# A start of its own for each pair's split weights, at every multiple of 4 bytes from 4 to 252

## The chip, the cores and the metric

The kernel runs on one core of one Trainium2 chip. The metric is device time in microseconds, from the first to the last instruction of one execution as the host sees it, as a median over runs.

## What is computed

The reference is a two-layer trunk on a sequence of 512 frames of width 1024, in float32. Each layer normalises x, projects it by one wide matrix, runs two recurrences in chunkwise form, merges them, and adds three residual blocks:

```
h  = rmsnorm(x, norm1_g);  z = h @ w_in + b_in            # 12296 columns
A  = sigmoid(mo) * headnorm(mlstm(q, k, v, i, f))         # 4 heads, dk = dv = 256
B  = silu(rg) * headnorm(retention(rope(rq), rope(rk), rv))   # 4 heads, dk = 256, dv = 512
x += (sigmoid(gm) * (A @ w_bm) + sigmoid(gr) * (B @ w_br)) @ w_out
x += relu(rmsnorm(x) @ w_ff1 + b_ff1)^2 @ w_ff2 + b_ff2
x += sigmoid(rmsnorm(x) @ w_pe_gate) * (p @ w_pe)
```

A last rmsnorm gives the output. Nearly all the arithmetic is dense products of a 1024-row weight matrix with the 512 frames.

## The kernel before, in words

**Three products for one.** Activations lie transposed, 128 features on the partitions and frames along the free axis. TensorE multiplies in a reduced form of float32 (float32r), so each operand is split in two: `hi`, the value as ScalarE writes it in that form, and `lo`, what is left, made by VectorE as the source minus `hi` (`split`, L308 to L310: L309 is ScalarE's part, L310 VectorE's). Each product is then three matmuls into one PSUM accumulation: hi by hi, hi by lo, lo by hi.

**Units.** The work is a list of units (`unit_list`), one per weight block, in a fixed order. There are three kinds that matter here:

- T8 units: a 1024 x 128 weight block, stationary, against all 512 frames. 8 feature blocks by 3 matmuls of 128 x 512 (`mm3`, L488 to L490).
- WIDE units: a 1024 x 1024 block in which the weights are the moving operand (L583 to L585).
- PAIR units, 75 of them: a 1024 x 256 block computed by one level of Strassen's scheme. It has 7 products, each of 4 feature blocks by 3 matmuls with the weights stationary and 256 frames or sums of frames moving: 84 matmuls of 128 x 256 (`run_pair`, L539 to L541). The weights of a pair come in four pieces: A, B and C of 1024 columns, D of 512.

The seventh product, P4 with piece D, is held back and issued in the middle of the next unit, after its second product.

**The feed.** Raw weights come by SyncE's DMA queue into one of 4 buffers `wr` (L413 to L428). Sums of weight blocks that the scheme needs are made beforehand in DRAM by accumulating DMAs on GpSimd's queue (L367), or by VectorE in the buffers (L467 to L474). `prep_next` (L431 to L475) takes a piece, splits it from `wr` into a tile `both` of the pool `w` (3 buffers; one more for D), and leaves two views of the tile, `hi` and `lo`, for TensorE. It runs a few pieces ahead of the products (`ready`).

**Where the split weights lie in their tile.** The tile is `2 * w + SLACK` words of 4 bytes per partition, with w = 1024 (512 for D) and `SLACK` = 64. The two views start `o` words in, and lie one behind the other:

```
both = pl.tile([P, 2 * w + SLACK], F32R, name=f"w{n}_{nm}", **kw)          # L443
o = 2 if units[n][0] == "PAIR" or pl is not wpool else 0                   # L444
out_ = [both[:, o + a * w:o + a * w + w] for a in range(1 if gates else 2)]
```

So pairs, and the last 4 units (which have 256 frames moving too), start 8 bytes into their tile, and all other units at its start. In the program as built every tile of split weights starts 32 bytes past a multiple of 64 in its partition, and so do the tiles of activations, of scores (`ph`, `pl`) and of values (`vh`, `vl`). A block of 128 weights is 512 bytes, so all blocks of one piece have the same distance from a multiple of 64.

Two other kinds of matmul have about 256 columns moving: the scores of the heads (`scores`, L817 to L836: tiles `l0m1s` and the like, in their shorter rows), and the product of scores and values of the mLSTM (`attend`, L838 to L845: `l0m2a`, `l0m3a`), with scores stationary and 258 columns of values moving. Values of two heads share a tile: head 2 starts at its word 0, head 3 at its word 258 (1032 bytes).

Of the kernel before, what the change touches and what calls it, by code (L numbers as in the profile page):

```python
# [124 lines left out]
def is_wide(g):  # L125
    return g[1][:2] in ("rv", "rw")
# [7 lines left out]
def has_t2(g):  # L134

    return is_full(g) or g[1][0] == "f"
# [117 lines left out]
def build(ctx, tc, ins, out):  # L254
    nc = tc.nc
    ve, ac, gp, te = nc.vector, nc.scalar, nc.gpsimd, nc.tensor
    units = [u for i in range(L) for u in unit_list(i)]
    NU = len(units)

    def pool(name, bufs, **kw):  # L260
        return ctx.enter_context(tc.tile_pool(name=name, bufs=bufs, **kw))

    def phase(name, side, bufs=1):
        return tc.alloc_tile_pool(name=name, bufs=bufs, side=side, reuse_waits="tile")
# [5 lines left out]
    wpool = pool("w", PIECES)  # L270
# [31 lines left out]
    def ps(name):  # L302
        return psum.tile([P, T], F32, name=name, tag="ps")

    def tmp(name, dt=F32):
        return cur["tmp"].tile([P, T], dt, name=name, tag="t", bufs=cur["ntmp"])

    def split(src, hi_ap, lo_ap):  # L308
        a = ac.activation(hi_ap, src, AF.Copy)  # L309
        return a, ve.tensor_sub(lo_ap, src, hi_ap.bitcast(F32))  # L310

    def in_order(kind, *new):

        for a, b in zip(cur.get(kind, ()), new):
            tc.add_manual_dep(b.ins, a.ins.name, ORDER, reason="order of the weights")
        cur[kind] = new
# [4 lines left out]
    for g, v in groups().items():  # L321
        index[g] = len(index)
        src, n, w = ("wwide", 2, UN) if is_wide(g) else ("wpairs", len(v), Q)
# [63 lines left out]
    def full(n):  # L387
        return units[n][0] in ("PAIR", "WIDE") and is_full(units[n][1])
# [10 lines left out]
    def halves(n):  # L399

        return [slice(0, Q), slice(Q, UN)] if n == 1 else [slice(0, UN)]

    def fill_raws(most=RAWS + 1):
        while at["load"] < len(loads) and len(raws) + len(kept) < most:
            n, x = loads[at["load"]]
            r = None
            if n in cur["room"] and cur["more"] not in raws:
                cur["more"] = n, x
                r = cur["low"].tile([P, UN], F32, name=f"wr{at['load']}", tag="wrx", bufs=1)
            elif len(raws) - (cur["more"] in raws) >= RAWS:  # L410
                break
            raws[n, x] = r = r or wpool.tile([P, UN], F32, name=f"wr{at['load']}", tag="wr", bufs=RAWS)
            if x:  # L413
                _, g, p = units[n]
                assert made.get((g, x[1] if is_wide(g) else p)) == 2 * len(MADE_OF(g)), (g, p, made, at["unit"])
                if is_wide(g):
                    in_order("load", nc.sync.dma_start(r, block(g, x[0])[x[1]]))
                else:
                    for k, y in enumerate(PIECE[x][:1] if x == "B" and not has_t2(g) else PIECE[x]):
                        in_order("load", nc.sync.dma_start(r[:, k * Q:(k + 1) * Q], block(g, y)[p]))  # L420
            elif units[n][0] == "IF":
                eng = nc.sync if n else nc.scalar
                eng.dma_start(r[:, 0:64], ins["wif"][n * L // NU])
            else:
                w = ins["wstream"][at["whole"]]
                for c in halves(n):
                    in_order("load", nc.sync.dma_start(r[:, c], w[:, c]))
                at["whole"] += 1  # L428
            at["load"] += 1

    def prep_next():  # L431
        n, x = order[at["prep"]]
        at["prep"] += 1
        fill_raws()

        w = Q if x == "D" else UN
        pl = cur["last"] if n >= NU - LAST else wpool
        kw = {"tag": "d", "bufs": 1} if x == "D" else {"tag": "l", "bufs": LAST} if pl is not wpool else {
            "tag": "w", "bufs": PIECES}
        wide = isinstance(x, tuple)  # L440
        nm = f"{x[0]}{x[1]}" if wide else x
        gates = units[n][0] == "IF"
        both = pl.tile([P, 2 * w + SLACK], F32R, name=f"w{n}_{nm}", **kw)  # L443
        o = 2 if units[n][0] == "PAIR" or pl is not wpool else 0  # L444
        out_ = [both[:, o + a * w:o + a * w + w] for a in range(1 if gates else 2)]
        r = formed.pop((n, x), None)
        if r is None:
            r = raws.pop((n, x))
        if gates:
            z = out_[0]  # L450
            gp.memset(z.bitcast(F32), 0.0)
            z = z.rearrange("p (k g c) -> p k g c", g=4, c=32)
            split(r[:, 0:64].rearrange("p (k g c) -> p k g c", g=2, c=H), z[:, :, 0:2, 0:H], z[:, :, 2:4, 0:H])
        elif x == 0:
            with tc.high_priority(AHEAD if n < 10 and units[n][0] == "V" or units[n][1:] == SOON else 0):
                for c in halves(n):
                    in_order("prep", *split(r[:, c], *[a[:, c] for a in out_]))
        else:
            in_order("prep", *split(r[:, :w], *out_))
        pieces[n, x] = out_  # L460
        if full(n) or not wide and x in ("A", "C") and has_t2(units[n][1]):
            pass
        elif x == "A" or wide and x[0] == "t2":
            kept[n, x] = r
        elif x == "C":

            ve.tensor_tensor(raws[n, "B"][:, Q:], kept.pop((n, "A"))[:, Q:], r[:, :Q], OP.add)  # L467
        elif x == "B":

            ve.tensor_tensor(r[:, :Q], r[:, :Q], r[:, Q:], OP.add)  # L470
            formed[n, "D"] = r
        elif wide and x[0] == "B21":
            t = cur["br"].tile([P, UN], F32, name=f"t4{n}_{x[1]}", tag=("ph", "pl")[x[1]])
            ve.tensor_tensor(t, kept.pop((n, ("t2", x[1]))), r, OP.add)  # L474
            formed[n, ("t4", x[1])] = t  # L475

    def ready(k):
        while at["prep"] < min(len(order), k + 1):
            prep_next()
# [12 lines left out]
    def t8(act, name):  # L492

        _, wh, wl = unit("T8")
        o = ps(name)
        for k in range(KT):
            s = slice(k * P, (k + 1) * P)
            mm3(o, wh[:, s], wl[:, s], act[0][k], act[1][k], k == 0, k == KT - 1)
            if k == 3:
                flush()  # L500
            if k in (2, 5):
                pace()
        return o
# [480 lines left out]
    for i in range(L):  # L984
        act_side, ph_side = ("right", "left") if i == 0 else ("left", "right")
        xa = n1.act
        if i:
            cur["low"] = phase(f"low{i}", ph_side)
            cur["tmp"], cur["ntmp"] = cur["low"], NTMP
            cur["room"] = range(i * NU // L, i * NU // L + room)  # L990
        cur["br"] = phase(f"br{i}", ph_side)
# [315 lines left out]
        for d in range(4):  # L1307
            o = t8(xa, f"l{i}m0z{d}") if d else oz
# [116 lines left out]
        for c in range(KT):  # L1425
# [4 lines left out]
            u = tmp(f"l{i}bml{c}")  # L1430
            nc.scalar.dma_start(u, bm_dram[i, c])
            o = t8(yr, f"l{i}br1{c}")
# [37 lines left out]
        for c in range(KT):  # L1470
            o = t8((mh, ml), f"l{i}wo{c}")
# [144 lines left out]
        for c in range(KT - LAST if last else KT):  # L1616
            o = t8(n3.act, f"l{i}pg{c}")
# [44 lines left out]
    for a, n in enumerate(nn):  # L1662
        for c in range(KT - LAST, KT):
            _, wh, wl = ws[c - KT + LAST]
            o = ps(f"pl{a}{c}")[:, :256]
# [21 lines left out]
    x_pool.release()  # L1687
    assert at["unit"] == NU and at["prep"] == len(order) and not pieces and not raws and at["load"] == len(loads) and not kept and not formed and at["step"] == len(steps)

# [117 lines left out]
```

## Time and profile before

| | |
|---|---|
| median of 3 runs | 2301.65 us (2300.31 to 2305.29) |
| the profiled execution | 2302.19 us |
| its span, first to last instruction | 2300.5 us |
| granted TensorE clock | 0.998 |
| DVE, ACT, POOL busy | 76%, 55%, 27% |

In a row of a timeline stand the start in us from the span's beginning, the duration in us, the engine, the line, the operation and what it writes and reads. Matmuls are pipelined and their ends are modelled, so the distance between two starts tells what one costs, and its duration doesn't. In a row of groups stand the line, engine, operation, output and inputs, shapes, count, then busy time in us and the mean of one in ns, then the idle time before them with what ended it. PEld is the loading of the stationary operand, which overlaps the matmul before.

### The profile page before, as it was taken

The numbers are of one execution on the slowest core, as the hardware profiler recorded it, in microseconds if no ns is written. First come the engines' busy times: TensorE is split into PE (matmuls) and PEld (weight loads), VectorE is DVE, ScalarE is ACT, GpSimd is POOL, SyncE is SP. The second block draws the span as 40 slices with busy tenths as digits, with TensorE's granted clock in tenths as the row PEclk, the third lists the DMA queues.
The fourth block names the chain that finished last, engine by engine and source line by source line (L and its number), as shares of the span: only waits on it lengthen the run. The fifth ranks groups of instructions, "written<-read, shape, count | busy, mean of one in ns | idle before, by whom it ended". The sixth has DMA issues, their size and how long they took to land.

```text
span 2300.5 us, 36407 instructions
## 1 busy us (share of the span) xinstructions
PE 2277.2 (99%) x13532; PEld 2020.8 (88%) x13532; DVE 1759.0 (76%) x2690; ACT 1266.5 (55%) x1835; POOL 616.2 (27%) x984
## 2 busy tenths in 40 slices
PE   9999999999999999999999999999999999999998
PEld 7888899888888899999888888988888888999997
DVE  7877767886676878788779687777867678787785
ACT  6766544554554546556557564445545446566564
POOL 3332222223124322223432332221232242111112
PEclk9999999999999999999999999999999999999999
DMA  6776787787789888888886768876877898878741
GB/s 211 189 195 175 243 234 215 209 235 211 233 228 268 220 229 229 239 239 210 227 227 183 196 177 250 232 213 220 228 221 208 244 266 217 246 233 232 236 161 56
DMA packets 187890, 499.33 MB, mean 217 GB/s; under 512 B 26352, under 2 KB 29808, under 8 KB 187712
## 3 DMA queue, kind: packets, MB, share of 16 engines
q0 software_dynamic: 57520, 188.53, 36.9%
q1 hardware_dynamic: 114496, 280.97, 36.2%
q10 hardware_dynamic: 15696, 27.50, 3.6%
q8 instruction: 106, 1.74, 0.3%
q14 instruction: 72, 0.59, 0.1%
HBM read 478.03 MB, written 194.51 MB: 292 GB/s over the span
## 4 chain that ended last, share of the span: by engine, by line
PE 85%; DVE 7%; ACT 2%; issue 2%; DMA 2%; POOL 1%; SPq 0%; DVEq 0%; ACTq 0%; POOLq 0%
PE l0f L488 1%; PE l0f L489 1%; PE l0f L490 1%; PE l0br L488 1%; PE l1br L488 1%; PE l1br L490 1%; PE l0br L490 1%; PE l1br L489 1%; PE l0br L489 1%; DVE w_B L310 1%; PE l1f L488 1%; PE l1f L490 1%; PE l1f L489 1%; DVE w_C L310 1%; PE l0pg L488 1%
## 5 line engine op out<-in xcount | busy, mean ns | idle before, releaser
L309 ACT ACTIVATE w<-wr 128x1024 fp32r<-128x1024 f32 (+1 forms) x193 | 199.7, 1042 | 125.9 <-issue 28.5
L310 DVE TENSOR_TENSOR w<-wr,w 128x1024 fp32r<-128x1024 f32 (+1 forms) x193 | 233.8, 1214 | 45.3 <-ACT w L309 44.7
L309 ACT ACTIVATE w_B<-wr 128x1024 fp32r<-128x1024 f32 x123 | 130.4, 1060 | 150.5 <-PE l0bm L490 13.1
L310 DVE TENSOR_TENSOR w_B<-wr,w_B 128x1024 fp32r<-128x1024 f32 x123 | 150.0, 1221 | 55.0 <-ACT w_B L309 54.5
L309 ACT ACTIVATE w_C<-wr 128x1024 fp32r<-128x1024 f32 x75 | 79.3, 1057 | 66.8 <-issue 9.6
L310 DVE TENSOR_TENSOR w_C<-wr,w_C 128x1024 fp32r<-128x1024 f32 x75 | 92.4, 1233 | 25.0 <-ACT w_C L309 21.0
L309 ACT ACTIVATE w_A<-wr 128x1024 fp32r<-128x1024 f32 x75 | 79.0, 1054 | 46.6 <-DMA wr<-wpairs 4.4
L310 DVE TENSOR_TENSOR w_A<-wr,w_A 128x1024 fp32r<-128x1024 f32 x75 | 91.6, 1222 | 14.2 <-ACT w_A L309 12.0
L309 ACT ACTIVATE w_t<-wr 128x1024 fp32r<-128x1024 f32 x56 | 59.1, 1059 | 61.8 <-PE l0g2va L585 6.3
L309 ACT ACTIVATE w_D<-wr 128x512 fp32r<-128x512 f32 x75 | 47.3, 631 | 81.6 <-DVE wr L470 26.7
L310 DVE TENSOR_TENSOR w_t<-wr,w_t 128x1024 fp32r<-128x1024 f32 x56 | 68.4, 1221 | 19.7 <-ACT w_t L309 19.1
L488 PE MATMUL l0f<-l0n2h,w 128*128 128x512 f32 x176 | 68.7, 390 | 0.0
L490 PE MATMUL l0f<-l0n2h,w 128*128 128x512 f32 x176 | 68.5, 389 | 0.0
L489 PE MATMUL l0f<-l0n2l,w 128*128 128x512 f32 x176 | 68.5, 389 | 0.0
L310 DVE TENSOR_TENSOR w_D<-wr,w_D 128x512 fp32r<-128x512 f32 x75 | 51.7, 689 | 15.1 <-ACT w_D L309 14.6
L367 POOL DMA_DIRECT2D s30t<-wpairs x24 | 16.8, 700 | 91.9 <-PE l1o20a L541 9.0
L490 PEld LDWEIGHTS l0f<-l0n2h,w 128*128 128x128 f32 x176 | 33.0, 188 | 7.0
L488 PEld LDWEIGHTS l0f<-l0n2h,w 128*128 128x128 f32 x176 | 33.0, 188 | 6.5
L489 PEld LDWEIGHTS l0f<-l0n2l,w 128*128 128x128 f32 x176 | 33.0, 188 | 6.4
L488 PE MATMUL l1f<-l1n2h,w 128*128 128x512 f32 x96 | 37.6, 391 | 0.0
L490 PE MATMUL l1f<-l1n2h,w 128*128 128x512 f32 x96 | 37.4, 390 | 0.0
L489 PE MATMUL l1f<-l1n2l,w 128*128 128x512 f32 x96 | 37.4, 389 | 0.0
(5796 smaller groups left out, 9085.3 us busy)
## 6 DMA issues: line engine op xcount, KB each, us to landing
wr<-wstream SPq DMA_DIRECT2D x189, 512.0 KB, 4.9
wr<-wpairs SPq DMA_DIRECT2D x225, 256.0 KB, 4.1
wr<-wwide SPq DMA_DIRECT2D x48, 512.0 KB, 4.6
s3t<-wwide POOLq DMA_DIRECT2D x24, 256.0 KB, 4.3
s6t<-wwide POOLq DMA_DIRECT2D x24, 256.0 KB, 5.2
s18t<-wwide POOLq DMA_DIRECT2D x24, 256.0 KB, 5.1
s21t<-wwide POOLq DMA_DIRECT2D x24, 256.0 KB, 5.1
s24t<-wpairs POOLq DMA_DIRECT2D x24, 256.0 KB, 5.7
```

The source lines that it names most:

```text
L309: a = ac.activation(hi_ap, src, AF.Copy)
L310: return a, ve.tensor_sub(lo_ap, src, hi_ap.bitcast(F32))
L367: dma = gp.dma_start(piece(g, x, p, q), piece(g, MADE[x][a], p, q), max_dma_last_dim=4096, **kw)
L488: te.matmul(o, sh, mh, start=first, stop=False)
L489: te.matmul(o, sh, ml, start=False, stop=False)
L490: cur["mm"] = te.matmul(o, sl, mh, start=False, stop=last)
```

## The change

The start `o` of a pair's pieces is no longer 2 for all pairs. The q-th pair of the program (counted from 0) takes `1 + 25 * q % 63`, that is 1 + ((25 q) mod 63) words: 1, 26, 51, 13, 38, 63, 25 and so on. The first 63 pairs take each whole number from 1 to 63 once, the last 12 take those of the first 12 again. All four pieces of a pair, hi and lo, share its start. The slack of 64 words already holds this, so tiles, buffers and addresses of all else stay where they were. On each engine the instructions and their order are the same, row for row.

```
@@ -256,6 +256,7 @@
     units = [u for i in range(L) for u in unit_list(i)]
     NU = len(units)
+    start_of = {n: 1 + 25 * q % 63 for q, n in enumerate(n for n, u in enumerate(units) if u[0] == "PAIR")}
@@ -441,7 +442,7 @@
         both = pl.tile([P, 2 * w + SLACK], F32R, name=f"w{n}_{nm}", **kw)
-        o = 2 if units[n][0] == "PAIR" or pl is not wpool else 0
+        o = start_of[n] if units[n][0] == "PAIR" else 2 if pl is not wpool else 0
         out_ = [both[:, o + a * w:o + a * w + w] for a in range(1 if gates else 2)]
```

Of the 75 starts 38 are odd numbers of words, and one (q = 58) is the 2 of before. Eight are multiples of 32 bytes, three of them of 64.

More of the change, by code (lines that the diff above doesn't have):

```diff
@@ L258, in build @@
     NU = len(units)
+    start_of = {n: 1 + 25 * q % 63 for q, n in enumerate(n for n, u in enumerate(units) if u[0] == "PAIR")}
     def pool(name, bufs, **kw):
@@ L443, in prep_next @@
         both = pl.tile([P, 2 * w + SLACK], F32R, name=f"w{n}_{nm}", **kw)
-        o = 2 if units[n][0] == "PAIR" or pl is not wpool else 0
+        o = start_of[n] if units[n][0] == "PAIR" else 2 if pl is not wpool else 0
         out_ = [both[:, o + a * w:o + a * w + w] for a in range(1 if gates else 2)]
```

## The prediction

> **What bounds the kernel now.** I read the page first (span, engines, chain), then timelines of TensorE, because what the change can touch is the step from one matmul's start to the next.
>
> ```profile
> span 2300.5 us, 36407 instructions
> PE 2277.2 (99%) x13532; PEld 2020.8 (88%) x13532; DVE 1759.0 (76%) x2690; ACT 1266.5 (55%) x1835; POOL 616.2 (27%) x984
> PEclk9999999999999999999999999999999999999999
> PE 85%; DVE 7%; ACT 2%; issue 2%; DMA 2%; POOL 1%; SPq 0%; DVEq 0%; ACTq 0%; POOLq 0%
> ```
>
> TensorE is busy 99% of the span at full clock and makes 85% of the chain that ended last. So the kernel is a row of matmuls end to end, and a nanosecond on each of the pairs' 75 x 84 = 6300 matmuls is 6.3 us, 0.27% of the time. About 0.2% (4.6 us) is what a measurement of this kernel can tell from no change. The profiled execution took 2302.19 us, its span and 1.7 us around it; the median of the runs is 2301.65, 0.02% less.
>
> What does a pair's matmul cost now? This is the timeline of TensorE at the first matmul of two pairs in a row, in a stretch without waits:
>
> ```profile
> 838.63 0.28 PE L539 MATMUL l0o02a<-l0hh,w_A 128*128 128x256 f32 x1
> ...
> 848.34 0.28 PE L539 MATMUL l0o03a<-l0hh,w_A 128*128 128x256 f32 x1
> ```
>
> Between the two lie 84 matmuls (72 of the one pair, and the 12 of P4 that the pair before left): 9.71 us / 84 = 115.6 ns. The last units, whose weights also start 8 bytes in, have the same step:
>
> ```profile
> 2267.77 0.28 PE L489 MATMUL pl<-l1n3l,w 128*128 128x256 f32 x1
> ...
> 2269.39 0.28 PE L488 MATMUL pl<-l1n3h,w 128*128 128x256 f32 x1
> ```
>
> 14 steps in 1.62 us: 115.7 ns. Weights at the tile's start with 512 frames moving:
>
> ```profile
> 129.09 0.39 PE L488 MATMUL l0m2z<-l0xnh,w 128*128 128x512 f32 x1
> ...
> 131.13 0.39 PE L488 MATMUL l0m2z<-l0xnh,w 128*128 128x512 f32 x1
> ```
>
> 9 steps in 2.04 us, 226.7 ns. The 256 columns more cost 111.1 ns, 0.43 ns a column. A load of weights has a price of its own, seen where the moving operand has only 2 columns (the last of these 8 matmuls runs between the two loads):
>
> ```profile
> 769.37 0.95 PE L710 MATMUL l0n2ss<-ones_r,l0n2sum 128*128 128x2 f32 x8
> ...
> 770.15 0.19 PEld L488 LDWEIGHTS l0f<-l0n2h,w 128*128 128x128 f32 x1
> 770.26 0.19 PEld L489 LDWEIGHTS l0f<-l0n2l,w 128*128 128x128 f32 x1
> ```
>
> Loads follow each other 110 ns apart there. So with 256 columns the moving stream (111) and the next load (110) are about equally long and run side by side, and the pairs' 115.6 is some 5 ns above either. Two streams that read SBUF at once and are both close to the bound: here a start can matter.
>
> **Does it, in this trace?** Two groups of matmuls, alike but for the distance between their two operands, answer. In both the scores are stationary, at 32 bytes past a multiple of 64, with 258 columns of values moving. The values of `l0m2a` start at 32 too; those of `l0m3a` start 1032 bytes later, so at 40.
>
> ```profile
> 205.00 0.28 PE L488 MATMUL l0m2a<-l0m1vh,l0m2ph 128*128 128x258 f32 x1
> ...
> 208.48 0.28 PE L490 MATMUL l0m2a<-l0m1vh,l0m2pl 128*128 128x258 f32 x1
> ...
> 240.82 0.28 PE L488 MATMUL l0m3a<-l0m1vh,l0m3ph 128*128 128x258 f32 x1
> ...
> 244.27 0.28 PE L490 MATMUL l0m3a<-l0m1vh,l0m3pl 128*128 128x258 f32 x1
> ```
>
> Each is 29 steps: 3.48 us or 120.0 ns with equal starts, 3.45 us or 119.0 ns with the weights 8 bytes behind the values. Less 0.9 ns for the 2 columns more that is 119.1 and 118.1 at 256 columns. The scores, equal starts and 256 columns, lie near that, though the stretch is short and follows longer rows:
>
> ```profile
> 118.80 0.28 PE L488 MATMUL l0m1s<-l0m1qh,l0m1kh 128*128 128x256 f32 x1
> ...
> 120.10 0.28 PE L490 MATMUL l0m1s<-l0m1qh,l0m1kl 128*128 128x256 f32 x1
> ```
>
> 11 steps in 1.30 us, 118.2 ns. So three distances of weights from moving operand have a price: 0 bytes 119.1 ns, 8 behind 118.1, 8 ahead (the pairs now) 115.6.
>
> **The change part by part.** Nothing is added, removed or moved in any engine's order; only addresses change, for three kinds of access.
>
> *ScalarE writes hi, VectorE reads hi and writes lo.* At the tile's start (group `w`, mostly T8) and at 8 bytes (`w_A`) the splits cost the same:
>
> ```profile
> L309 ACT ACTIVATE w<-wr 128x1024 fp32r<-128x1024 f32 x189 | 198.1, 1055 | 125.9 <-issue 28.5 <-PE l0m1vp L809 10.3 <-PE l1m1vp L809 10.3
> L309 ACT ACTIVATE w_A<-wr 128x1024 fp32r<-128x1024 f32 x75 | 79.0, 1054 | 46.6 <-DMA wr<-wpairs 4.4 <-PE l0bm L490 4.4 <-issue 3.9
> L310 DVE TENSOR_TENSOR w<-wr,w 128x1024 fp32r<-128x1024 f32 x189 | 232.0, 1230 | 45.3 <-ACT w L309 44.7
> L310 DVE TENSOR_TENSOR w_A<-wr,w_A 128x1024 fp32r<-128x1024 f32 x75 | 91.6, 1222 | 14.2 <-ACT w_A L309 12.0 <-PE l0r1brqa L541 0.7 <-PE l1r1brqa L541 0.7
> L1043 DVE SCALAR_TENSOR_TENSOR l0m00cv<-l0m00z,bc,l0m00cv x3: 741/743/743, 50.8 to 53.5; 128x511 f32<-128x511 f32 x1, 128x510 f32<-128x510 f32 x1, 128x509 f32<-128x509 f32 x1
> ```
>
> Odd starts on VectorE are in the trace too: the convolution's taps read and write 1, 2 and 3 words in, and take 741 to 743 ns, the odd ones no more than the even. I take 0 for the splits. ScalarE at an odd start is not shown; VectorE's row is the nearest, and bounds it at 0.
>
> [...]
>
> How much it waits is in the answer for line 541, among what its engine sat idle for:
>
> ```profile
>   DVE w_B L310: 4.3, 10
> ```
>
> 10 times, 4.3 us. If splits got slower, this is the wait that grows, and behind it stand TensorE's in-order matmuls of that pair; at the price of 0 it doesn't. If TensorE gets slower it shrinks: 10 pairs in which a slower TensorE is partly given back.
>
> *TensorE loads the weights.* The term that counts. A pair is 84 loads, so 1 ns is 0.084 us for a pair. By kind of start:
>
> - The one pair with the old start: 0.
> - Eight pairs start at a multiple of 32 bytes. That the pattern repeats after 32 bytes isn't shown; after 16 it would be 17 pairs, after 64 three. I take the middle. Price of equal starts: 119.1 - 115.6 = 3.5 ns, x 84 = 0.29 us; eight: 2.4 us.
> - The other 66, odd ones included. Their starts are in no row. The nearest are the two unequal ones, 115.6 and 118.1. I take the middle, 116.9, since neither is nearer: +1.25 ns, 0.105 us a pair, 6.9 us in all.
> - Given back in the 10 pairs that wait for splits: about 1.0 us.
>
> Sum: 2.4 + 6.9 - 1.0 = 8.3 us, 2302.2 + 8.3 = 2310.5 us for a profiled execution, and 0.02% less as a median: **2310 us**. The ends of the unknown price: if all 74 pairs cost what equal starts cost, 74 x 0.29 = 22 us, 2323. If all unknown starts are as good as 8 bytes ahead, 2.4 us, 2304. Below nothing: the load alone needs 110 ns, so up to 5 ns of the step could go.
>
> **The rivals.**
>
> *No change that can be told (within 4.6 us).* Only equal starts hurt, and anything else is like 8 bytes ahead: 2.4 us, 2304 us (1 us with three such pairs, 5 with 17). For it: 8 bytes is enough for most of the difference. Against it: 8 bytes behind gains only 1.0 of the 3.5 ns.
>
> *Faster.* Some starts let load and stream pass without hindrance. If half the 74 pairs fell to the middle between 115.6 and 110, 112.8 ns: 37 x 84 x 2.8 = 8.7 us, 2293 us. It decides if the mean step of all pairs falls by more than 0.7 ns. For it: 115.6 is above both streams alone, so there is something to gain. Against it: of three distances known, the present one is the lowest.
>
> [...]
>
> *The change doesn't do what it says:* excluded by reading; 63 words and 2 x 1024 fit in the tile's 2112.
>
> **How the numbers follow.** The forecast, slower by a few tens of us at most, gets 0.56; slower by far 0.08; no change 0.25; faster 0.11. So slower 0.64, same 0.25, faster 0.11. The range starts at 2298, which takes in no change and the near half of faster, and ends at 2330, above every pair at the price of equal starts (2323) and with a little for odd starts; it leaves out about 0.08 above and 0.06 below.
>
> **What would show it.** Steps of pairs in stretches without waits, pair by pair: the one with the old start at 115.6, those at multiples of 32 bytes near 119, the others between 115.6 and 118.1, and no more for odd starts. Steps of T8 units stay at 226.7, rows of `w_A` on ScalarE and VectorE at 1054 and 1222 ns, and the waits for `w_B` at or below 4.3 us. I am wrong if other starts step below 115 ns, if odd starts step beyond 120, or if the splits get longer.

## The result and the profile after

The changed kernel takes 2316.08 us, median of 3 runs (2314.42 to 2316.81), against 2301.65 before (2300.31 to 2305.29): a ratio of 1.0057, with a 95% interval of 1.0044 to 1.0071. It is slower by 14.4 us, more than the 8.3 forecast, and inside the range of 2298 to 2330. (In experiment 10 below, one of eleven executions had a granted clock of 0.393 and took 7916.18 us; its ratio and its range are those of the other ten.) The two profiled spans differ by 2312.7 - 2300.5 = 12.2 us, and those 12.2 us are what the traces can account for.

The page of the changed kernel, in the rows that were shown of before:

```profile
span 2312.7 us, 36407 instructions
PE 2293.3 (99%) x13532; PEld 2037.7 (88%) x13532; DVE 1760.3 (76%) x2690; ACT 1266.4 (55%) x1835; POOL 614.9 (27%) x984
PEclk9999999999999999999999999999999999999999
PE 88%; DVE 6%; ACT 2%; issue 2%; DMA 1%; POOL 1%; SPq 0%; DVEq 0%; ACTq 0%; POOLq 0%
```

The clock and the count of instructions are the same. TensorE is busy 16.1 us more and its weight loads (PEld) 16.9 us more, VectorE 1.3 us more, ScalarE 0.1 us less. TensorE's share of the chain rose from 85 to 88%: it waits less for the others.

The splits, in the answer of groups by shape (busy us, then the mean of one in ns):

```profile
L310 ACT ACTIVATE w<-wr 128x1024 fp32r<-128x1024 f32 x189 | 198.2, 1055 | 127.9 <-issue 28.5 <-PE l1m1vp L810 10.3 <-PE l0m1vp L810 10.3
L310 ACT ACTIVATE w_A<-wr 128x1024 fp32r<-128x1024 f32 x75 | 79.0, 1053 | 47.0 <-PE l1bm L491 4.4 <-PE l0bm L491 4.4 <-issue 3.9
L311 DVE TENSOR_TENSOR w_A<-wr,w_A 128x1024 fp32r<-128x1024 f32 x75 | 91.7, 1223 | 12.8 <-ACT w_A L310 11.0 <-PE l0r1brqa L542 0.7 <-DMA wr<-s1t 0.7
```

1053 and 1223 ns where 1054 and 1222 stood: 38 of these 75 pieces now start at an odd word, and neither engine took notice. What TensorE's third matmul of a triple sat idle for, in the answer for its line:

```profile
  DVE w_B L311: 2.1, 7
```

10 waits of 4.3 us (L541 in the kernel before) became 7 of 2.1 us (L542). Now the steps. In TensorE's timeline of the changed kernel, 48 matmuls lie between the two rows of each couple: `l0o02` starts 23 words in, `l0o03` 48, `l1o00` 16 words. The last couple is a T8 unit, 10 matmuls of 512 columns apart.

```profile
845.67 0.28 PE L540 MATMUL l0o02a<-l0hh,w_B 128*128 128x256 f32 x1
...
851.42 0.28 PE L540 MATMUL l0o03a<-l0hh,w_A 128*128 128x256 f32 x1
...
855.67 0.28 PE L540 MATMUL l0o03a<-l0hh,w_B 128*128 128x256 f32 x1
...
861.32 0.28 PE L540 MATMUL l0f11a<-l0n2h,w_A 128*128 128x256 f32 x1
...
1970.28 0.28 PE L540 MATMUL l1o00a<-l1hh,w_B 128*128 128x256 f32 x1
...
1975.72 0.28 PE L540 MATMUL l1o01a<-l1hh,w_A 128*128 128x256 f32 x1
...
128.45 0.39 PE L491 MATMUL l0m2z<-l0xnh,w 128*128 128x512 f32 x1
...
130.71 0.39 PE L489 MATMUL l0m2z<-l0xnh,w 128*128 128x512 f32 x1
```

119.8, 117.7 and 113.3 ns where each of these pairs had 115.6, and 2.26 us / 10 = 226 ns in the T8 unit, unchanged. So pairs with different starts now step differently, on both sides of the old step, and far more often slower than faster.

**Where the 12.2 us are.** Every distance from one matmul's start to the next in the two traces, added up: the pairs' matmuls took 744.4 us before and 756.9 after, the 512-column matmuls 1417.1 and 1416.6. All of the difference is in the pairs. Counting steps of 135 ns and more as waits, the mean step without waits went from 115.74 to 118.48 ns, 2.75 before rounding, x 6300 = 17.3 us more. The waits inside pairs (what those long steps have beyond a mean step) went from 15.25 to 10.42 us, 4.8 us less. 17.3 - 4.8 = 12.5.

### The profile page after: what moved, and what is told of

Read it like the earlier page. It is cut to its first block, busy times and chain, and to the rows that moved or that the text cites. A ratio compares the mean times of both kernels' runs of the same rounds, so it can differ in the third digit from the quotient of the medians.

```text
span 2312.7 us, 36407 instructions
## 1 busy us (share of the span) xinstructions
PE 2293.3 (99%) x13532; PEld 2037.7 (88%) x13532; DVE 1760.3 (76%) x2690; ACT 1266.4 (55%) x1835; POOL 614.9 (27%) x984
## 4 chain that ended last, share of the span: by engine, by line
PE 88%; DVE 6%; ACT 2%; issue 2%; DMA 1%; POOL 1%; SPq 0%; DVEq 0%; ACTq 0%; POOLq 0%
PE l0br L489 1%; PE l1br L490 1%; PE l0br L490 1%; PE l1br L489 1%; PE l1br L491 1%; PE l0br L491 1%; PE l0f L489 1%; PE l0f L491 1%; PE l0f L490 1%; PE l1f L489 1%; PE l1f L491 1%; PE l1f L490 1%; PE l0pg L489 1%; PE l0pg L491 1%; PE l0bm L490 1%
## 5 line engine op out<-in xcount | busy, mean ns | idle before, releaser
L311 DVE TENSOR_TENSOR w_B<-wr,w_B 128x1024 fp32r<-128x1024 f32 x123 | 150.1, 1222 | 55.0 <-ACT w_B L310 54.6
L310 ACT ACTIVATE w_A<-wr 128x1024 fp32r<-128x1024 f32 x75 | 79.0, 1053 | 47.0 <-PE l1bm L491 4.4
L311 DVE TENSOR_TENSOR w_A<-wr,w_A 128x1024 fp32r<-128x1024 f32 x75 | 91.7, 1223 | 12.8 <-ACT w_A L310 11.0
L311 DVE TENSOR_TENSOR w_t<-wr,w_t 128x1024 fp32r<-128x1024 f32 x56 | 68.4, 1222 | 19.4 <-ACT w_t L310 18.9
L368 POOL DMA_DIRECT2D s30t<-wpairs x24 | 16.8, 701 | 92.9 <-PE l1o11a L542 9.5
```

The costliest lines, as they stand in the source:

```text
L368: dma = gp.dma_start(piece(g, x, p, q), piece(g, MADE[x][a], p, q), max_dma_last_dim=4096, **kw)
```

## The experiments

Two theories. *Start alone*: the distance between weights and moving operand sets the step. *Start and history*: one start allows more than one step, and what came before picks it. Rivals to both: the place of the weights, or the splits that write them, and not the distance. All kernels but that of experiment 5 are the changed kernel with the lines shown edited. Steps are means over a pair without waits, from the starts in the trace.

**1. All pairs 16 words in.** In the changed kernel that was one of the lowest steps, seen in one pair.

```
-        o = start_of[n] if units[n][0] == "PAIR" else 2 if pl is not wpool else 0
+        o = 16 if units[n][0] == "PAIR" else 2 if pl is not wpool else 0
```

> All 75 pairs start 16 words (64 bytes) in. Start alone (each start has a step of its own, whatever the pair): every pair steps at 113.4 to 113.7 ns, as the one pair with this start did in the changed kernel; 6300 x -1.9 ns = -12 us, 2290 us. Start and history (a start allows several repeating patterns of steps, and the disturbance before picks one): pairs without waits spread by over 2 ns, some near 113.4, some near 119 to 120 as the other starts at multiples of 64 bytes had; 2295 to 2320 us. Only the distance modulo 64 bytes counts: like start 0, all near 119, 2323 us.

Measured: 2304.93 us, ratio 1.0015 (1.0005 to 1.0024). Two steps and nothing between, in stretches without waits. TensorE's timeline, twice 48 matmuls of one kernel with one start:

```profile
847.28 0.28 PE L540 MATMUL l0o02a<-l0hh,w_B 128*128 128x256 f32 x1
...
852.93 0.28 PE L540 MATMUL l0o03a<-l0hh,w_A 128*128 128x256 f32 x1
...
928.79 0.28 PE L540 MATMUL l0o12a<-l0hh,w_B 128*128 128x256 f32 x1
...
934.23 0.28 PE L540 MATMUL l0o13a<-l0hh,w_A 128*128 128x256 f32 x1
```

5.65 us / 48 = 117.7 ns, and 5.44 / 48 = 113.3. In this trace the step changes only at a wait or where one unit gives way to the next. The pieces A, B and C of a pair lie in different buffers, and the step stays the same through all of them, so the buffer doesn't pick it here. The start does not settle it alone: history it is, for this start.

**2. All pairs 22 words in**, the other low start of the survey (the same line, with 22).

> All 75 pairs start 22 words (88 bytes) in. Start alone: every pair at 113.4 ns after its first few matmuls, as the one pair with this start had; 6300 x -2.1 ns = -13 us, 2289 us. Start and history: some pairs at 113.4 and some at 117 to 120; 2295 to 2315 us. Distance modulo 16 bytes decides (88 is 8 past a multiple of 16, as the 8 bytes of before): all at 115.6, 2302 us.

Measured: 2299.15 us, ratio 0.9983 (0.9974 to 0.9992): faster than both kernels. Most pairs step at 113.3 ns, eight at 116.5 to 116.7 (the fifth, sixth, ninth and tenth of each layer); the mean is 114.1. The pairs' matmuls take 735.6 us, 8.8 less than before, where (115.74 - 114.09) x 6300 would be 10.4: a faster TensorE waits more (16.8 us inside pairs for 15.25). These figures are of the profiled execution, at 2294.38 us the fastest of the ten; the median is 3.5 us below the kernel before, not 8.8.

**3. All pairs at the tile's start** (the same line, with 0), the equal starts that the forecast priced at 119.1 ns.

> All 75 pairs start at their tile's start, with weights and moving operand equally placed modulo 64 bytes. The price of equal starts that the prediction used: 119.1 ns in every pair, +3.5 x 84 x 75 = +22 us, 2323 us. Start alone with the period of 64 bytes: as the starts of 16, 32 and 48 words did in the changed kernel (113.7, 119.7, 117.8), so a mean near 117, +9 us, 2311 us. Start and history: pairs spread between 113.4 and 120.

Measured: 2323.53 us, ratio 1.0092 (1.0077 to 1.0107). TensorE's timeline:

```profile
845.63 0.28 PE L540 MATMUL l0o02a<-l0hh,w_B 128*128 128x256 f32 x1
...
851.39 0.28 PE L540 MATMUL l0o03a<-l0hh,w_A 128*128 128x256 f32 x1
```

5.76 us / 48 = 120.0 ns, and every pair lies at 119.5 to 120.0 (standard deviation 0.11 ns; 1.87 with 16 words). This start shows one step in all 75 pairs, whatever came before. So does the start of the kernel before, 2 words: 115.5 to 116.5 ns in all 75 pairs, standard deviation 0.21. The forecast's end for it, 2323 us, holds. And 0 and 16 words, both multiples of 64 bytes, differ (119.5 to 120.0 against 113.3 and 117.7 ns): nothing repeats after 32 or 64 bytes.

**4. A second survey**, the same 63 starts dealt to other pairs.

```
-    start_of = {n: 1 + 25 * q % 63 for q, n in enumerate(n for n, u in enumerate(units) if u[0] == "PAIR")}
+    start_of = {n: 1 + (25 * q + 31) % 63 for q, n in enumerate(n for n, u in enumerate(units) if u[0] == "PAIR")}
```

> The same 63 starts, given to other pairs: pair q takes 1 + (25 q + 31) mod 63 words. Start alone: the step of a start is that of the changed kernel within 0.5 ns for over 50 of 63 starts, and the time is 2316 us within 3 us. Start and history: for at least a third of the starts the step differs by over 1 ns between the two kernels, while the time is still near 2316 us (2311 to 2321), since the mean over 63 starts changes little. The pair alone, not the start: the differences go with the pair, and the steps of each pair stay as in the changed kernel.

Measured: 2316.0 us, ratio 1.0062 (1.0045 to 1.0079), as slow as the changed kernel. The step in ns for starts of 0 to 63 words, first survey / second:

```
 0:      -       118.3/118.3  116.0/115.7  116.8/116.8  118.3/118.2  117.2/119.9  121.5/120.3  117.2/116.6
 8: 118.4/118.3  119.8/119.7  119.0/118.9  117.8/117.9  118.3/118.1  118.9/113.5  117.8/117.8  119.5/119.6
16: 113.7/113.7  118.4/118.4  118.3/118.4  115.6/117.7  118.7/118.7  120.0/119.9  113.7/114.4  119.6/118.5
24: 118.0/118.6  119.9/119.8  119.7/119.5  121.2/119.6  119.8/119.6  119.0/119.1  119.2/118.8  119.9/119.1
32: 119.7/119.9  119.5/118.8  118.0/118.0  119.8/119.8  119.2/118.2  116.8/116.7  117.1/117.5  119.6/119.7
40: 119.8/119.7  117.5/117.7  119.9/119.9  117.0/118.8  118.0/118.1  117.6/113.9  117.7/117.9  118.2/118.2
48: 117.8/117.7  118.4/118.2  118.5/118.4  119.9/116.5  116.8/116.9  117.4/117.4  119.3/119.7  120.5/120.6
56: 116.6/116.7  119.8/119.9  117.9/118.0  119.7/119.7  118.0/117.3  119.7/119.3  117.9/117.7  120.0/120.1
```

47 of 63 starts agree within 0.5 ns, ten differ by more than 1 (5, 6, 13, 19, 23, 27, 36, 43, 45 and 51 words). That is under the 50 expected of *start alone*, and the ten fall short of the third of 63 expected of *start and history*. By start the two surveys correlate at 0.74, by pair at -0.04. The start mostly decides and the pair doesn't; a minority of starts has a choice. The old start, 2, is among the lowest of all 63, and only 16 and 22 lie clearly below it in both.

**5. The tiles moved, not the start.** This is the kernel before, all pairs at 2 words, with one line edited: the padding of the program's rows, which sets where later tiles lie, is 40 for 48. (It moves the T8 units' distances too, so the total says nothing about pairs.)

```
-PAD = 48
+PAD = 40
```

> The kernel before (all pairs 8 bytes in) with the pad 8 words shorter, which moves the tiles of weights and part of the moving operands down by 32 bytes, and leaves other moving operands where they are. So all weights lie at another place, and their distance to the moving operand is 8 bytes in some pairs, as before (in layer 0 the 16 pairs of the second feed-forward product), and -24 bytes, 58 words modulo 256 bytes, in others (the same 16 pairs of layer 1). Distance decides: steps of 115.6 ns in those of layer 0, and near 118.0 in those of layer 1, as both surveys gave for a start of 58 words. The place of the weights alone decides: 118.0 in both. Splits at another place decide, or nothing but the old place matters: the same step in both layers. The total isn't predicted, since T8 units get other distances too.

Measured: one run, 2324.78 us. The weights of layer 0's second feed-forward product (`l0o`) lie 8 bytes ahead of the moving operand as before; those of layer 1 (`l1o`) 24 bytes behind it. A start of 58 words is 232 bytes, the same distance if distances 256 bytes apart count as one. TensorE's timeline, 48 matmuls of each:

```profile
850.45 0.28 PE L539 MATMUL l0o02a<-l0hh,w_B 128*128 128x256 f32 x1
...
856.00 0.28 PE L539 MATMUL l0o03a<-l0hh,w_A 128*128 128x256 f32 x1
...
2001.39 0.28 PE L539 MATMUL l1o02a<-l1hh,w_B 128*128 128x256 f32 x1
...
2007.04 0.28 PE L539 MATMUL l1o03a<-l1hh,w_A 128*128 128x256 f32 x1
```

115.6 and 117.7 ns; the surveys have 117.9 and 118.0 for 58 words. The start within the tile, and with it the splits' writes, is the same in both, so neither of these makes the step: the distance to the moving operand does. The pairs of the first feed-forward product lie the other way round, 24 bytes behind in layer 0 (118.1 to 118.3 ns) and 8 ahead in layer 1 (115.7 to 116.1), so it isn't the layer either. Three pairs of `l1o` in a row, 24 bytes behind like the others, stepped at 121.6 to 123.3. That stays unexplained.

**6. The other units surveyed.** Pairs at 2 words; 512-column units that started at 0 take the 63 starts instead. The forecast said that a start can matter because at 256 columns the load (110 ns) and the stream (111 ns) are level. At 512 columns a step is 226.7 ns, and they aren't.

```
-    start_of = {n: 1 + 25 * q % 63 for q, n in enumerate(n for n, u in enumerate(units) if u[0] == "PAIR")}
+    start_of = {n: 1 + 25 * q % 63 for q, n in enumerate(n for n, u in enumerate(units) if u[0] not in ("PAIR", "IF") and n < NU - LAST)}
...
-        o = start_of[n] if units[n][0] == "PAIR" else 2 if pl is not wpool else 0
+        o = start_of.get(n, 0 if units[n][0] == "IF" else 2)
```

> The survey on the other side: pairs stay 8 bytes in, and every T8, V, PE and WIDE unit (512 columns in each matmul) gets a start of its own out of 1 to 63 words. If it is the level race of load and stream in matmuls of 256 columns alone that makes the start count, steps at 512 columns stay within 1 ns of 226.7, and the time within 6 us of 2302. If each load takes its price from the stream it runs beside, whatever its length, T8 steps rise by 1 to 4 ns as the pairs' did: about 5800 matmuls, +6 to +20 us.

Measured: one run, 2329.17 us against 2301.05 of the kernel before beside it. TensorE's timeline in the T8 unit shown before, now 10 words in:

```profile
128.98 0.40 PE L489 MATMUL l0m2z<-l0xnh,w 128*128 128x512 f32 x1
...
131.08 0.39 PE L489 MATMUL l0m2z<-l0xnh,w 128*128 128x512 f32 x1
```

9 steps in 2.10 us, 233.3 ns for 226.7. Over all 4080 matmuls of T8 units the mean rose from 227.1 to 232.0 ns, over the 1728 with the weights moving from 226.9 to 233.1: together 20.0 + 10.7 = 30.7 us, against 28 measured. So the start matters though the load, 110 ns of the 226.7, has over 100 ns to spare, and the forecast's reason falls. What is more, equal starts are among the best there (in the means by start of T8 units, 226.7 to 235.8 ns, only 30 and 60 words match them) and among the worst at 256 columns. A start can have more than one step here, too: 10 words, 233.3 ns in the unit shown, stepped at 226.7 and 226.8 in two other units.

**7. All pairs 13 words in and 8. all pairs 45 words in** (the same line, with 13 and 45): two odd starts on which the surveys disagreed by 5.4 and 3.7 ns.

> All pairs 13 words in, a start that stepped at 120.1, 117.6 and 113.5 ns in the three pairs that had it. Start and history: steps sit at 113.3 or at 120 and change between them only at waits or changes of unit; mean between, time 2295 to 2325 us. Start alone (its three values being chance): one step of about 117 in all pairs, 2311 us.

> All pairs 45 words in, a start that stepped at 117.6 and 113.9 ns in the two pairs that had it. Start and history: pairs at 113.3 and at 117 to 118, changing only at disturbances; 2290 to 2315 us. Start alone: one step in all, near 116, 2304 us. An odd start has no price of its own: the low step of 113.3 ns is reached at this odd start as at 16 and 22 words.

Measured: 2307.64 us, ratio 1.0023 (1.001 to 1.0035), with 13; 2303.6 us, 1.001 (1.0 to 1.0019), with 45. TensorE's timeline with 13 words, two pairs of one layer:

```profile
845.82 0.28 PE L540 MATMUL l0o02a<-l0hh,w_B 128*128 128x256 f32 x1
...
851.26 0.28 PE L540 MATMUL l0o03a<-l0hh,w_A 128*128 128x256 f32 x1
...
1008.00 0.28 PE L540 MATMUL l0o22a<-l0hh,w_B 128*128 128x256 f32 x1
...
1013.76 0.28 PE L540 MATMUL l0o23a<-l0hh,w_A 128*128 128x256 f32 x1
```

113.3 and 120.0 ns; with 45 words it is 113.3 or 118.2. Both have two steps, and both reach the lowest step seen at any start: an odd start has no price of its own.

**9. A mix**, 22 words but 13 in the eight pairs that stepped at 116.7 in experiment 2 and at 113.3 to 114 with 13 in experiment 7, timed over 5 rounds; and **10. 22 words once more**, the same kernel as experiment 2, beside it.

```
-    start_of = {n: 1 + 25 * q % 63 for q, n in enumerate(n for n, u in enumerate(units) if u[0] == "PAIR")}
+    start_of = {n: 13 if q in (4, 5, 8, 9, 39, 40, 43, 44) else 22 for q, n in enumerate(n for n, u in enumerate(units) if u[0] == "PAIR")}
```

> 22 words for all pairs but the eight that the run with 22 everywhere held at 116.7 ns (the 5th, 6th, 9th and 10th pair of each layer), which take 13, at which they stepped at 113.4 to 113.9. Start and history, with the state set by the start and the kind of unit before: the eight fall to about 113.7, 8 x 84 x 3.0 ns = 2.0 us below 22 for all, 0.3% below the kernel before, 2295 us. If history reaches across units of another kind, so that new neighbours set other states, some pairs sit at 116 to 120 again and nothing is gained over 22 for all (2299 us).

> 22 words for all pairs once more, to stand beside the mix on the same chip. It was 0.17% faster than before, with 0.08 to 0.26 as interval; the same again within 0.1%. In the first run the pairs' mean step fell by 1.6 ns, which is 10 us, but the median time by only 3.5 us, with single runs 7 us apart: if the state of the steps differs from run to run, the spread of the runs is again over twice that of the kernel before.

Measured: the mix 2297.7 us, ratio 0.9982 (0.9973 to 0.9991); 22 words again 2298.59 us, 0.9983 (0.9974 to 0.9992). The eight pairs fell to 113.4 to 113.9 as meant, but in the mix's profiled execution other pairs sat at 116 to 120 ns, and the two kernels can't be told apart. Experiments 2 and 10 are one kernel. TensorE's timeline at the same 48 matmuls, first of experiment 2:

```profile
1001.32 0.28 PE L540 MATMUL l0o22a<-l0hh,w_B 128*128 128x256 f32 x1
...
1006.75 0.28 PE L540 MATMUL l0o23a<-l0hh,w_A 128*128 128x256 f32 x1
```

and of experiment 10, from the place where it took another step:

```profile
990.83 0.28 PE L540 MATMUL l0o20a<-l0hh,w_D 128*128 128x256 f32 x1
...
992.08 0.28 PE L542 MATMUL l0o20a<-l0hh,w_D 128*128 128x256 f32 x1
992.21 0.36 PE L540 MATMUL l0o21a<-l0hh,w_B 128*128 128x256 f32 x1
992.40 0.28 PE L541 MATMUL l0o21a<-l0hl,w_B 128*128 128x256 f32 x1
...
998.04 0.28 PE L540 MATMUL l0o22a<-l0hh,w_A 128*128 128x256 f32 x1
...
1002.36 0.28 PE L540 MATMUL l0o22a<-l0hh,w_B 128*128 128x256 f32 x1
...
1008.12 0.28 PE L540 MATMUL l0o23a<-l0hh,w_A 128*128 128x256 f32 x1
```

11 steps in 1.25 us up to 992.08: 113.6 ns. Then one matmul is held for 0.19 us, and 47 steps from 992.40 to 998.04 take 5.64 us: 120.0 ns, kept through the next pair (5.76 us / 48) where experiment 2 had 113.1. Same program, same addresses, another step, entered at a delay of under 0.1 us. The two executions ran on different chips, but the change from 113.6 to 120.0 lies within one execution, at one start. That is history seen at work. It may also be what widens the runs, though no run isolates it: the 22-word kernel ranges over 8.3 us in ten executions, the one before beside it over 4.6 in 21. That is 1.8 times as much, less than the twice that was expected.

## Why the prediction was right in sign and short in size

- **Which engine.** Right: only TensorE's steps in the pairs moved. Splits, clock, order and the T8 units stayed.
- **Splits at 0.** Right on ScalarE too, which the trace of before didn't show: 1053 against 1054 ns, and 1223 against 1222 on VectorE, over pieces of which half start odd. Each of their rows is one long run of 1024 words: from an odd start these took 1055 ns on ScalarE and 1223 on VectorE, from an even one 1052 and 1222.
- **Equal starts at 119.1 ns.** Right in size (119.9, experiment 3), but wrong as the price of the eight multiples of 32 bytes: these lie from 113.7 to 119.8, on average 2.0 ns above before, 8 x 84 x 2.0 = 1.4 us for the 2.4 forecast. No period of 32 or 64 bytes shows.
- **The other 66 starts at the middle of two rows.** This is the step that failed. +1.25 ns was forecast, +2.87 measured: 66 x 84 x 2.87 = 15.9 us for 6.9. The two rows were good as rows (2 words 116.0 and 115.7; 62 words, 8 bytes behind, 117.9 and 117.7). But one of them is the present start, which is among the lowest of 63, so the middle lay between a rare low and the typical. Of the 66 pairs one fell below 115.6, 23 lay within the stated 115.6 to 118.1, and 42 above.
- **Given back.** 4.8 us for 1.0. The forecast saw only the waits for `w_B`, which gave 2.2. The other half came from waits of the pairs' first and second matmuls, for operands that VectorE and ScalarE write, which also arrive in time when TensorE runs late (the second matmuls' 3 waits for `l1hl`, 1.6 us before, are none now). So two errors of opposite sign partly cancelled, and that the sum came as near as it did is partly luck: 1.4 + 15.9 - 4.8 = 12.5, for 8.3 forecast.
- **The reason.** "Load and stream about level" is not what makes a start matter: experiment 6 shows the price with twice the columns (227.1 to 232.0 ns in T8 units). The sign came out right because the present start is among the lowest, which the forecast knew only against two other distances.
- **The rivals.** *No change* fell with the 2.87 ns. *Faster* was wrong for this mix of starts, but starts below 115.6 exist (16 and 22 words, 113.7 ns), and experiment 2 is that kernel; that load and stream pass without hindrance there was the author's guess, and no run shows it. *Slower by far*, the 0.08 above 2330 us, fell, and no run shows odd starts to be the dear ones: odd ones rose by 3.05 ns, even ones that aren't multiples of 32 bytes by 2.63, and the three highest steps are both odd (27 and 55 words, 121.2 and 120.5) and even (6 words, 121.5). Two of the signs set for being wrong came: steps under 115 ns (16 and 22 words) and odd starts beyond 120.

**What stays open.** Why one distance between the weights and the moving operand costs more than another, and why some starts have more than one step (22 words showed 113.3, 116.7 and 120.0), isn't settled by any run. That distances 256 bytes apart count as one is borne out for two distances only: 24 bytes behind (experiment 5, 117.7 ns where 58 words had 117.9 and 118.0), and 8 bytes ahead, where in the program as built the distances within a pair differ by multiples of 256 bytes and all 75 pairs of the kernel before step alike (115.5 to 116.5 ns).

## What to carry to other kernels

In this kernel, with TensorE busy 99% of the span, the distance between the stationary and the moving operand in SBUF was a knob: 113.3 to 121.5 ns a matmul of 256 columns in the surveys and experiments 1 to 3, 226.7 to about 236 at 512, at no cost in instructions (36407 before and after). Survey it at the size in question, over all starts, before setting it: two rows of a trace, of which one is the tuned value, say little about the typical start, and equal starts were among the best at one size and among the worst at the other. Then try the best few on all units and time them often, since a start can hold more than one step (13 words: 113.3 and 120.0 ns); 22 words for all pairs beat both kernels here, at 0.9983 (0.9974 to 0.9992) in each of two timings.

## What was not expected of the hardware

- Steps of matmuls with one start can lock at 113.3 or at 120.0 ns (22 and 13 words; 22 also at 116.7) and keep that: 131 steps of 120.0 ns in a row from 992.40 to 1008.12 us in experiment 10, after 113.6 before a delay of under 0.1 us.
- Some starts showed a single step through all 75 pairs: 119.5 to 120.0 ns at 0 words, 115.5 to 116.5 at 2.
- 512-column matmuls lost some 5 ns on average by unequal starts (227.1 to 232.0 in T8 units, experiment 6), though a load (110 ns) takes less than half of their time.
